# A hybrid decoder trunk: a reordered recurrence stage, a gate row broadcast by DMA, and a new spread of the conditioning products

## The chip, the cores and the metric

The kernel runs on one core of one Trainium2 chip. The metric is the device time of one execution in microseconds (us), the median of several executions. A core has five engines that this text names as the profile does: TensorE (PE, with its weight loads shown as PEld), VectorE (DVE), ScalarE (ACT), GpSimd (POOL) and SyncE (SP). In this kernel SP issues the transfers from memory; its queue is shown as SPq. Engines run side by side, each takes its own instructions strictly in the order of the compiled program, and they wait for each other through semaphores.

## The reference

Two layers are applied to a sequence of 256 tokens with 1024 features. Each layer has three sub-layers: a half-step SwiGLU FFN, a token mixer, and another half-step FFN. The mixer of layer 0 is HGRN2, a gated linear recurrence; that of layer 1 is a chunked causal gMLP. So there are six stages: ffn0, hg, ffn1, ffn2, gm, ffn3.

```python
def sublayer(x, fn, pre_g, post_g, shift, scale, gate, res_w):
    h = rms_norm(x, pre_g) * (1.0 + scale) + shift
    return x + res_w * gate * rms_norm(fn(h), post_g)

def swiglu(h, w_in, w_out):
    a, b = jnp.split(h @ w_in, 2, axis=-1)
    return (jax.nn.silu(a) * b) @ w_out

# HGRN2: q, f, i, g = split(h @ w_in); 8 heads of 128
#   f = lb + (1-lb) sigmoid(f), k = 1 - f, S_t = diag(f_t) S_{t-1} + k_t i_t^T, o_t = S_t^T silu(q_t)
#   out = (rms_norm(o per head) * silu(g)) @ w_out
```

The shift, scale and gate vectors of all stages come from `silu(c) @ ada_w`: per stage 24 columns of 128 features, 144 in all. The kernel computes each column as one product over a 128x1024 slab of `ada_w`; these are the conditioning products.

## The kernel before

The activations stay on chip, the weights (float32) are streamed once. Every weight block is 128x2048 and comes in two halves of 512 KB. `wblock` (L111 to L124) issues the two loads, ScalarE casts each half to a high part (L118) and VectorE subtracts it to get a low part (L119); TensorE then computes each product as three passes, high by high, high by low and low by high. There are twelve slots for these 128x2048 tiles (`whl`), four for raw halves.

`next_block` (L126) hands out the blocks in one fixed order and loads ahead by `self.ahead` blocks. The loads are kept in program order on SP's queue. `pace` (L133) spreads the conditioning products over the loads: `pace(upto, blocks)` lets each following block issue the same share of the products that are missing to `upto`. The table `bgs` (L925) has the count to which each stage goes. A product is a 512 KB load into one of the two slots of the pool `adap` (L165, L166) and one multiply-and-sum on VectorE (L168). `pre_cols` (L172) and `gate_tile` (L187) issue at once what is still missing of the columns that they read.

`gate_tile` (L187 to L200) makes G, the gate times the post-norm weight, as a 128x1024 tile with the same row in every partition: eight TensorE transposes of a broadcast column (L197) into two PSUM banks and two ScalarE copies (L199). `tail` (L248) uses G at the end of the stage (L257, L261).

An FFN stage runs units of hidden features (`unit`, L310), each from two blocks, with an output block behind (`out_unit`, L331), then the last three output blocks (`out_last`, L337) and the tail, in which the normalisation of the next stage begins. `ffn` calls `G_fn` at u == 8 of 11.

The stage hg (`hgrn`, L447) is written out by hand. `feat` (L455) projects 512 features with features on partitions, in four steps; `tok` (L472) projects 512 features with tokens on partitions, in four steps; `gate_f` (L486) turns a forget projection into decay sums with exponentials and logarithms, and borrows the slots of `adap` for its work tile L (L488). `attn` (L513) handles four heads: diagonal scores (L521), seven levels of halving, each with scaled copies X (L544 to L555), a set of score matmuls (L561) and a masked merge (L532), and then the output matmuls (L594, L596). `finish` (L601) normalises the outputs of four heads. `zip_steps` (L657) puts steps of other work between the steps of `attn` as fill for TensorE. The order before is: output gate of half 0 and values of half 0 together; queries of half 0; forget gate of half 0; G; queries of half 1 and one step of the forget gate of half 1 ahead; `attn(0)` beside the rest of that and the values of half 1; `attn(1)` beside the output gate of half 1, `finish(0)` and half of the output projection; then the silu of the second output gate, `finish(1)` and the tail. `self.gate` (L564) makes the next fill matmul follow the last score matmul in TensorE's order; `table` (L70) switches ScalarE's function table.

Of the kernel before, what the change touches and what calls it, by code (L numbers as in the profile page):

```python
# [10 lines left out]
F32 = mybir.dt.float32  # L11
# [4 lines left out]
ALU = mybir.AluOpType  # L16
# [17 lines left out]
class Body:  # L34
    def __init__(self, ctx, tc, ins, out):
        self.ctx, self.tc, self.nc, self.out = ctx, tc, tc.nc, out
        self.d = dict(zip(_INS, ins))
        pool = lambda name, bufs, **k: ctx.enter_context(tc.tile_pool(name=name, bufs=bufs, **k))
        self.const = pool("const", 1)
        self.raw = pool("raw", 4)  # L40
        self.whl = pool("whl", 12)
        self.act = pool("act", 1)
        self.adap = pool("adap", 2)
        self.cols = pool("cols", 2)
        self.tiny = pool("tiny", 4)
# [5 lines left out]
        self.yps = pool("yps", 1, space=PSUM)  # L51


    def load(self, out, src):
# [132 lines left out]
    def gate_tile(self, s, res_w):  # L187
        nc = self.nc
        self.ada(24 * s + 24)
        g = self.cols.tile([P, KC], F32, tag="gate", name="gate")  # L190
        nc.vector.tensor_add(g, self.mod[s][:, 16:24], self.adab[:, 24 * s + 16:24 * s + 24])
        nc.vector.scalar_tensor_tensor(g, g, res_w, self.npost[:, s, :], op0=ALU.mult, op1=ALU.mult)
        G = self.act.tile([P, D], F32, tag="G", name="G")
        for h in range(2):
            ps = self.acc.tile([P, 512], F32, tag="acc", name="gps")
            for k in range(4):
                nc.tensor.transpose(ps[:, k * P:(k + 1) * P], g[:, 4 * h + k:4 * h + k + 1].to_broadcast([P, P]),  # L197
                                    self.ident)
            nc.scalar.copy(G[:, h * 512:(h + 1) * 512], ps)  # L199
        return G  # L200


# [244 lines left out]
    def hgrn(self, hT, G_fn, pre_next, nxt, bg):  # L447
# [65 lines left out]
        def attn(hb, bank, res):  # L513
# [86 lines left out]

        def finish(hb, ops, sqrt=False):  # L601
            ss = self.tiny.tile([P, 8], F32, tag="ss8", name="ss8")
            o4 = [o.rearrange("p t h v -> p (t h) v") for o in ops]
            for u in range(2):
                for i in range(4):
                    junk = self.scr.tile([P, 512], BF16, tag="junka", name="junka")
                    nc.scalar.activation(junk[:, 0:P], o4[u][:, i, :], AF.Square, accum_out=ss[:, 4 * u + i:4 * u + i + 1])
            nc.vector.tensor_scalar(ss, ss, 1.0 / P, EPS, op0=ALU.mult, op1=ALU.add)
            r = self.tiny.tile([P, 8], F32, tag="r8", name="r8")
            if sqrt:  # L610
                self.tact(ss, ss, AF.Sqrt)
                nc.vector.reciprocal(r, ss)
# [1 line left out]
                self.rsqrt(r, ss)  # L614
            for u in range(2):
                pair = 2 * hb + u
                on = self.t2().rearrange("p (i v) -> p i v", i=4)
                for i in range(4):
                    t, c0 = i // 2, (2 * pair + i % 2) * P
                    nc.vector.scalar_tensor_tensor(on[:, i, :], o4[u][:, i, :], r[:, 4 * u + i:4 * u + i + 1],  # L620
                                                   gg[:, t, c0:c0 + P], op0=ALU.mult, op1=ALU.mult)
# [18 lines left out]
        def bank_a():  # L640
            return self.acc.tile([P, 512], F32, tag="acc", name="ab")

        def g_silu(g):
            o = gg[:, :, g * 512:(g + 1) * 512]
            self.tact(o, o, AF.Silu)

        def once(fn):
            fn()
            return
            yield  # L650

        def run(*gens):
            for gen in gens:
                for _ in gen:
                    pass
# [20 lines left out]
        v = self.wtile(F32).rearrange("p (t c) -> p t c", t=NT)  # L676
# [3 lines left out]
        kn, bq = [], [self.wtile(F32), self.wtile(F32)]  # L680
        qs = lambda hb, pr: bq[hb][:, H4 + 512 * pr:H4 + 512 * pr + 512]
        run(feat(lambda pr, ps: self.tact(qs(0, pr), ps, AF.Silu)))
        kn.append(self.wtile(F32))
# [4 lines left out]
        def q1_silu():  # L688
            self.table("silu_and_others")
            self.tact(bq[1][:, H4:], bq[1][:, H4:], AF.Silu)  # L690
            self.table("natural_log_exp_and_others")
        self.ahead = 1
        kn.append(self.wtile(F32))
        ops, oTs = [[], []], []
        G = G_fn()
        zip_steps(attn(0, bank_y, ops[0]), [
            feat(lambda pr, ps: nc.scalar.copy(qs(1, pr), ps)), once(q1_silu),
            feat(lambda pr, ps: gate_f(1, pr, ps)),
            tok(lambda t, ps: nc.scalar.copy(v[:, t, 512:], ps))], 5)
        self.ahead = 1  # L700
        oall = []
        y = None

        def outs():
            finish(0, ops[0])
            yield
            y = self.y_banks()
            state["y"] = y
# [11 lines left out]
        self.table("silu_and_others")  # L720
        g_silu(1)
        pre_next()
        self.table("sqrt_and_others")
        finish(1, ops[1], True)
# [190 lines left out]
    def run(self):  # L915
# [57 lines left out]
def _blk(w, rows, cols):  # L973

    r0, nr = rows
    c0, ncol = cols
    return w[r0:r0 + nr, c0:c0 + ncol].reshape(nr // P, P, ncol).transpose(1, 0, 2).reshape(P, -1)


def _layout(i):  # L980
# [35 lines left out]
    L["wffn"] = np.stack(wf)  # L1016
    hw, ho = a["hg_w_in"][0], a["hg_w_out"][0]
    bl = []
    for c0 in (3072, 2048, 0, 1024, 512, 1536, 2560, 3584):
        bl += [_blk(hw, (512 * h, 512), (c0, 512)) for h in range(2)]  # L1020
# [37 lines left out]
```

## Time and profile before

| what | value |
|---|---|
| median of 3 runs | 1213.34 us (1212.44 to 1213.79) |
| the profiled execution | 1208.2 us, its span from first to last instruction 1206.4 us |
| mean granted TensorE clock | 0.986 |
| TensorE busy | 1161.2 us, 96% of the span |
| VectorE busy | 858.4 us, 71% |
| ScalarE busy | 627.7 us, 52% |
| read from memory | 276.97 MB, 230 GB/s over the span |

A row of a windows view gives the stretch in us from the start of the span, its length, then for each engine the busy time with the number of instructions in brackets, then the granted clock (1.00 is full), the busy share of the DMA engines and the rate in GB/s. A row of waits names who waited, for whom, the total in us, how often and the longest. A row of the timeline gives start and length in us, engine, line, operation, and in square brackets the idle time before and what ended it. Matmuls overlap, so the distance of two starts is what one costs.

### The profile page before, as it was taken

The page shows a single profiled execution, that of the slowest core. Times are in us where ns is not written, and L with a number is a line of the kernel's source. Part 1 is how long each engine was busy: PE and PEld are TensorE (multiplying, and loading weights), DVE is VectorE, ACT ScalarE, POOL GpSimd, SP SyncE. Part 2 cuts the span into 40 slices and gives each one's busy share as a digit, 9 for nine tenths or more (in the row PEclk, how much of TensorE's full clock was granted, in tenths as well). Part 3 has the DMA queues.
Part 4 walks back from the last instruction along what each step waited for, and adds up shares of the span by engine and source line. Part 5 has one row for each costly group of instructions (what it writes and reads, how often), then busy time and mean ns, then how long its engine had stood idle before and what let it go on. Part 6 is the DMA issues. An engine that isn't in the chain of part 4 may idle for free.

```text
span 1206.4 us, 18818 instructions
## 1 busy us (share of the span) xinstructions
PE 1161.2 (96%) x7424; PEld 1042.9 (86%) x7424; DVE 858.4 (71%) x1223; ACT 627.7 (52%) x925; POOL 0.2 (0%) x4
## 2 busy tenths in 40 slices
PE   7999999999988999998899999999999999999997
PEld 6999997898876999986789999888888887999996
DVE  6998788879878877767766455466878787755632
ACT  6454446669576433334754344454654457534431
POOL 0000000000000000000000000000000000000000
PEclk9999999999998999998899999999999999999999
DMA  9888988863345888888667666436777665766630
GB/s 354 303 299 328 346 307 310 279 228 130 102 143 176 293 309 295 303 290 270 209 206 231 210 222 200 160 123 237 243 244 248 223 213 192 249 209 206 228 104 35
DMA packets 78714, 279.25 MB, mean 231 GB/s; under 512 B 9633, under 2 KB 10273, under 8 KB 78626
## 3 DMA queue, kind: packets, MB, share of 16 engines
q1 hardware_dynamic: 78626, 278.05, 67.7%
q8 instruction: 58, 0.95, 0.3%
q14 instruction: 30, 0.25, 0.1%
HBM read 276.97 MB, written 1.05 MB: 230 GB/s over the span
## 4 chain that ended last, share of the span: by engine, by line
PE 64%; DMA 17%; DVE 9%; ACT 5%; issue 4%; SPq 1%; DVEq 0%; ACTq 0%
DMA raw<-in_wffn 11%; PE ups L322 9%; PE ups L324 9%; PE ups L323 9%; PE y L141 6%; PE y L143 6%; PE y L142 6%; PE ups L389 4%; DVE w L119 3%; DMA ada<-in_ada 3%; ACT w L118 2%; DMA raw<-in_whg 2%; DVE junkv L168 2%; PE pps L289 2%; PE pps L290 2%
## 5 line engine op out<-in xcount | busy, mean ns | idle before, releaser
L118 ACT CAST w<-raw 128x1024 fp32r<-128x1024 f32 x376 | 389.1, 1049 | 385.7 <-DMA raw<-in_wffn 153.6
L119 DVE TENSOR_TENSOR w<-raw,w 128x1024 fp32r<-128x1024 f32 x376 | 454.2, 1222 | 168.1 <-ACT w L118 157.1
L322 PE MATMUL ups<-hhi,w 128*128 128x256 f32 x1280 | 363.4, 284 | 0.8 <-ACT w L118 0.7
L324 PE MATMUL ups<-hhi,w 128*128 128x256 f32 x1280 | 362.1, 283 | 1.1 <-DVE w L119 1.1
L323 PE MATMUL ups<-hlo,w 128*128 128x256 f32 x1280 | 361.8, 283 | 0.0
L322 PEld LDWEIGHTS ups<-hhi,w 128*128 128x128 f32 x1280 | 245.3, 192 | 3.0 <-ACT w L118 1.5
L323 PEld LDWEIGHTS ups<-hlo,w 128*128 128x128 f32 x1280 | 245.3, 192 | 1.7 <-issue 0.2
L324 PEld LDWEIGHTS ups<-hhi,w 128*128 128x128 f32 x1280 | 245.2, 192 | 1.6 <-DVE w L119 1.6
L168 DVE CUSTOM_DVE_ANT_0 junkv<-ada,cond 128x1024 bf16<-128x1024 f32 x144 | 175.8, 1221 | 44.5 <-DMA ada<-in_ada 43.5
L141 PE MATMUL y<-w,t 128*128 128x512 f32 x448 | 181.0, 404 | 2.0 <-ACT w L118 1.2
L142 PE MATMUL y<-w,t 128*128 128x512 f32 x448 | 179.9, 402 | 2.8 <-DVE w L119 2.8
L143 PE MATMUL y<-w,t 128*128 128x512 f32 x448 | 179.3, 400 | 0.1
L142 PEld LDWEIGHTS y<-w,t 128*128 128x128 f32 x448 | 85.2, 190 | 23.6 <-DVE w L119 5.6
L141 PEld LDWEIGHTS y<-w,t 128*128 128x128 f32 x448 | 85.6, 191 | 21.4 <-ACT w L118 1.9
L143 PEld LDWEIGHTS y<-w,t 128*128 128x128 f32 x448 | 85.4, 191 | 20.6 <-DVE t L147 0.4
L289 PE MATMUL pps<-w,hhi 128*128 128x512 f32 x160 | 65.2, 407 | 5.9 <-DVE hhi L245 5.9
L290 PE MATMUL pps<-w,hhi 128*128 128x512 f32 x160 | 64.2, 402 | 0.0
L355 DVE TENSOR_TENSOR t<-t,ups 128x512 f32<-128x512 f32 x38 | 25.9, 685 | 31.5 <-PE ups L324 31.3
L146 ACT CAST t<-t 128x512 fp32r<-128x512 f32 x50 | 30.8, 618 | 29.0 <-DVE t L355 24.9
L292 PE MATMUL pps<-w,hlo 128*128 128x512 f32 x160 | 43.2, 391 | 0.0
L289 PEld LDWEIGHTS pps<-w,hhi 128*128 128x128 f32 x160 | 31.0, 194 | 13.9 <-DVE hhi L245 3.8
L324 PE MATMUL fps<-hhi,w 128*128 128x256 f32 x128 | 36.5, 285 | 1.7 <-DVE w L119 1.7
(190 smaller groups left out, 1215.7 us busy)
## 6 DMA issues: line engine op xcount, KB each, us to landing
raw<-in_wffn SPq DMA_DIRECT2D x264, 512.0 KB, 5.5
ada<-in_ada SPq DMA_DIRECT2D x144, 512.0 KB, 6.0
raw<-in_wgmu SPq DMA_DIRECT2D x48, 512.0 KB, 5.1
raw<-in_whg SPq DMA_DIRECT2D x40, 512.0 KB, 6.0
raw<-in_wgmv SPq DMA_DIRECT2D x24, 512.0 KB, 4.5
t<-in_gbin SPq DMA_DIRECT2D x6, 256.0 KB, 5.1
x<-in_x SPq DMA_DIRECT2D x2, 512.0 KB, 4.1
out<-x SPq DMA_DIRECT2D x4, 256.0 KB, 2.0
```

Of the source, the lines that this page charges most:

```text
L118: nc.scalar.copy(hi[:, sl], raw)
L119: nc.vector.tensor_sub(lo[:, sl], raw, hi[:, sl])
L141: self.paced(mm(ps, l[0], r[0], start=start, stop=False))
L142: mm(ps, l[0], r[1], start=False, stop=False)
L143: mm(ps, l[1], r[0], start=False, stop=stop)
L168: nc.vector.tensor_tensor_reduce(junk, t, self.cond, 1.0, 0.0, ALU.mult, ALU.add, self.mod[i // 24][:, i % 24:i % 24 + 1])
L289: mm(res[g][t], h(0, kc), u(0, kc), start=kc == 0, stop=False)
L290: mm(res[g][t], h(0, kc), u(1, kc), start=False, stop=False)
L322: self.paced(mm(o, u[0], h[0], start=start, stop=False))
L323: mm(o, u[0], h[1], start=False, stop=False)
L324: mm(o, u[1], h[0], start=False, stop=stop)
L389: nc.tensor.matmul(res[i][:, c * S:(c + 1) * S], wb[u // 2][:, c0:c0 + P], hT[u % 2][:, :, kc, :], start=kc + c + u == 0, stop=kc == KC - ...
```

## The change

Three parts.

1. `gate_tile` transposes the 128x8 gate once into 8x128, copies it to SBUF, writes it as 4 KB to a tile in device memory and reads it back with a broadcast to 128 partitions; both transfers are issued by GpSimd.
2. In `hgrn`, both halves of the output gate are projected first, then the forget gate of half 0, then both halves of the queries; the values of half 0 become fill (two steps ahead of `attn(0)`, two inside it), beside the whole forget gate of half 1 and one step of the values of half 1, whose other three steps go beside `attn(1)`. `G_fn` moves behind `attn(0)`. `once` now takes one step of a generator. The fill is also ordered behind the diagonal scores. `outs` has one more empty step behind `finish(0)`. `finish` squares a whole bank at a time, multiplies outputs and gate from PSUM on VectorE, sums the squares there and scales by the norm at the end. The silu of the second output gate and two table switches at the end of the stage are gone, and the blocks of `whg` are laid out in the new order.
3. `bgs` becomes 46, 64, 92, 118, 138, 144 (it was 48, 64, 112, 120, 136, 144).

```diff
+        ps = self.acc.tile([P, 512], F32, tag="acc", name="gps")
+        nc.tensor.transpose(ps[0:KC, 0:P], g, self.ident)
+        row = self.cols.tile([KC, P], F32, tag="grow", name="grow")
+        nc.scalar.copy(row, ps[0:KC, 0:P])
+        flat = self.dram.tile([KC, P], F32, tag="gflat", name="gflat")
+        nc.gpsimd.dma_start(flat, row)
         G = self.act.tile([P, D], F32, tag="G", name="G")
-        for h in range(2):
-            ps = self.acc.tile([P, 512], F32, tag="acc", name="gps")
-            for k in range(4):
-                nc.tensor.transpose(ps[:, k * P:(k + 1) * P], g[:, 4 * h + k:4 * h + k + 1].to_broadcast([P, P]),
-                                    self.ident)
-            nc.scalar.copy(G[:, h * 512:(h + 1) * 512], ps)
+        nc.gpsimd.dma_start(G, flat.rearrange("k p -> (k p)").unsqueeze(0).to_broadcast([P, D]))
...
-                    nc.tensor.matmul(ps[:, i * P:(i + 1) * P], k[:, c], q[:, c], start=True, stop=True)
+                    score = nc.tensor.matmul(ps[:, i * P:(i + 1) * P], k[:, c], q[:, c], start=True, stop=True)
+                self.gate = score
...
+            og = self.t4()
             for u in range(2):
-                for i in range(4):
-                    junk = self.scr.tile([P, 512], BF16, tag="junka", name="junka")
-                    nc.scalar.activation(junk[:, 0:P], o4[u][:, i, :], AF.Square, accum_out=ss[:, 4 * u + i:4 * u + i + 1])
+                o3 = ops[u].rearrange("p t h v -> p (t h) v")
+                sq = self.t2().rearrange("p (i v) -> p i v", i=4)
+                nc.scalar.activation(sq, o3, AF.Square)
+                c0 = 2 * (2 * hb + u) * P
+                nc.vector.tensor_mul(og[:, 512 * u:512 * u + 512].rearrange("p (t c) -> p t c", t=NT),
+                                     ops[u].rearrange("p t h v -> p t (h v)"), gg[:, :, c0:c0 + 2 * P])
+                nc.vector.reduce_sum(ss[:, 4 * u:4 * u + 4], sq, axis=mybir.AxisListType.X)
...
-                    nc.vector.scalar_tensor_tensor(on[:, i, :], o4[u][:, i, :], r[:, 4 * u + i:4 * u + i + 1],
-                                                   gg[:, t, c0:c0 + P], op0=ALU.mult, op1=ALU.mult)
+                    nc.vector.tensor_scalar(on[:, i, :], on[:, i, :], r[:, 4 * u + i:4 * u + i + 1], None, op0=ALU.mult)
...
         for t in range(NT):
-            self.tact(gg[:, t, 0:512], pg[0][t], AF.Silu)
-            nc.scalar.copy(v[:, t, 0:512], pg[1][t])
+            for g in range(2):
+                self.tact(gg[:, t, 512 * g:512 * g + 512], pg[g][t], AF.Silu)
...
-        run(feat(lambda pr, ps: self.tact(qs(0, pr), ps, AF.Silu)))
...
         run(feat(lambda pr, ps: gate_f(0, pr, ps)))
+        self.table("silu_and_others")
+        for hb in range(2):
+            run(feat(lambda pr, ps: self.tact(qs(hb, pr), ps, AF.Silu)))
+        self.table("natural_log_exp_and_others")
...
+        val = lambda i: tok(lambda t, ps: nc.scalar.copy(v[:, t, 512 * i:512 * i + 512], ps))
+        v0, v1 = val(0), val(1)
+        zip_steps(attn(0, bank_y, ops[0]), [
+            once(v0), once(v0), feat(lambda pr, ps: gate_f(1, pr, ps)), v0, once(v1)], 2)
         G = G_fn()
-        zip_steps(attn(0, bank_y, ops[0]), [
-            feat(lambda pr, ps: nc.scalar.copy(qs(1, pr), ps)), once(q1_silu),
-            feat(lambda pr, ps: gate_f(1, pr, ps)),
-            tok(lambda t, ps: nc.scalar.copy(v[:, t, 512:], ps))], 5)
...
             finish(0, ops[0])
+            yield
             yield
...
-        zip_steps(attn(1, bank_a, ops[1]), [
-            tok(lambda t, ps: nc.scalar.copy(gg[:, t, 512:], ps)), outs()], 0)
+        zip_steps(attn(1, bank_a, ops[1]), [v1, outs()], 0)
         y = state["y"]
-        self.table("silu_and_others")
-        g_silu(1)
...
-        bgs = {"ffn0": 48, "hg": 64, "ffn1": 112, "ffn2": 120, "gm": 136, "ffn3": 144}
+        bgs = {"ffn0": 46, "hg": 64, "ffn1": 92, "ffn2": 118, "gm": 138, "ffn3": 144}
```

More of the change, by code (lines that the diff above doesn't have):

```diff
@@ L51, in __init__ @@
         self.yps = pool("yps", 1, space=PSUM)
+        self.dram = pool("dram", 2, space=bass.MemoryType.DRAM)
     def load(self, out, src):
@@ L602, in finish @@
             ss = self.tiny.tile([P, 8], F32, tag="ss8", name="ss8")
-            o4 = [o.rearrange("p t h v -> p (t h) v") for o in ops]
+            r = self.tiny.tile([P, 8], F32, tag="r8", name="r8")
+            og = self.t4()
             for u in range(2):
-                for i in range(4):
-                    junk = self.scr.tile([P, 512], BF16, tag="junka", name="junka")
-                    nc.scalar.activation(junk[:, 0:P], o4[u][:, i, :], AF.Square, accum_out=ss[:, 4 * u + i:4 * u + i + 1])
+                o3 = ops[u].rearrange("p t h v -> p (t h) v")
[5 more added lines that the diff above has]
+                nc.vector.reduce_sum(ss[:, 4 * u:4 * u + 4], sq, axis=mybir.AxisListType.X)
             nc.vector.tensor_scalar(ss, ss, 1.0 / P, EPS, op0=ALU.mult, op1=ALU.add)
-            r = self.tiny.tile([P, 8], F32, tag="r8", name="r8")
             if sqrt:
@@ L641, in bank_a, with once @@
             return self.acc.tile([P, 512], F32, tag="acc", name="ab")
[L643 to L650, printed above, removed]
+        def once(gen):
+            yield next(gen)
         def run(*gens):
@@ L715, in outs @@
                     yield
-        zip_steps(attn(1, bank_a, ops[1]), [
-            tok(lambda t, ps: nc.scalar.copy(gg[:, t, 512:], ps)), outs()], 0)
+        zip_steps(attn(1, bank_a, ops[1]), [v1, outs()], 0)
         y = state["y"]
-        self.table("silu_and_others")
-        g_silu(1)
         pre_next()
@@ L1018, in _layout @@
     bl = []
-    for c0 in (3072, 2048, 0, 1024, 512, 1536, 2560, 3584):
-        bl += [_blk(hw, (512 * h, 512), (c0, 512)) for h in range(2)]
+    for c0, h in ((3072, 0), (3072, 1), (3584, 0), (3584, 1), (1024, 0), (1024, 1), (0, 0), (0, 1), (512, 0), (512, 1),
+                  (2048, 0), (1536, 0), (1536, 1), (2048, 1), (2560, 0), (2560, 1)):
+        bl.append(_blk(hw, (512 * h, 512), (c0, 512)))
     bl += [_blk(ho, (256 * u, 256), (0, D)) for u in range(4)]
```

11 lines of the change are left out of this document (3 added, 8 removed).

## The prediction

> **What bounds the kernel now.** I read the page first, then stretches of 20 us, then who waits where TensorE falls behind, and last the load queue, which stands behind most of it.
>
> ```profile
> span 1206.4 us, 18818 instructions
> 440.00:460.00 20.00, 20.00 (x147) 18.91 (x146) 14.84 (x20) 7.43 (x8) 0.00 (x0) 1.00 0.84 285
> 560.00:580.00 20.00, 16.78 (x53) 10.80 (x52) 14.79 (x15) 14.27 (x16) 0.00 (x0) 0.83 0.80 268
> 340.00:360.00 20.00, 17.85 (x107) 15.21 (x106) 16.39 (x18) 16.15 (x30) 0.00 (x0) 1.00 0.57 185
> 360.00:380.00 20.00, 15.62 (x64) 11.95 (x64) 14.27 (x29) 11.34 (x24) 0.00 (x0) 0.83 0.46 158
> ```
>
> The first row under the span is how most of the kernel looks: TensorE without a gap at full clock. So the time is the sum of TensorE's matmuls and the places where it starves. The other rows are the two places: the end of ffn1 (560 to 580) and the end of hg (340 to 380). In both the granted clock falls to 0.83 as well.
>
> The price of the first place can be read directly. Here are the output matmuls that close ffn1 and, below, the same 96 in ffn2:
>
> ```profile
> 553.20:592.30 39.10, 30.41 (x96) 20.69 (x96) 2.05 (x3) 2.03 (x6) 0.83 0.69 230
> 763.00:786.60 23.60, 22.84 (x96) 17.78 (x96) 2.05 (x3) 2.07 (x6) 1.00 0.37 120
> ```
>
> 39.1 against 23.6 us: ffn1 loses **15.5 us** that ffn2 does not lose. The stages compute the same; what differs is the conditioning products, 112 - 64 = 48 against 120 - 112 = 8. The load queue's own waits in the steady part, ffn1 first, then ffn2:
>
> ```profile
> SPq L55 <- DVE mod L168: 54.6, 32, 2.8
> SPq L55 <- DMA ada<-in_ada: 38.7, 24, 3.6
> ...
> SPq L55 <- DVE w L119: 108.0, 47, 4.5
> ```
>
> ```profile
> 407.00:540.00 133.00, 132.89 (x950) 124.73 (x947) 99.37 (x136) 50.23 (x59) 0.00 (x0) 1.00 0.88 299
> 622.00:755.00 133.00, 133.00 (x954) 125.31 (x953) 77.19 (x84) 56.87 (x68) 0.00 (x0) 1.00 0.67 218
> ...
> raw<-in_wffn SPq DMA_DIRECT2D x40, 512.0 KB, 7.3
> ada<-in_ada SPq DMA_DIRECT2D x36, 512.0 KB, 5.3
> ```
>
> In ffn2 the queue waits for weight slots: it is ahead. In ffn1 it never waits for those; it stands behind a product's load, whose two slots are still landing or being multiplied: 54.6 + 38.7 = 93.3 us for the 36 products of these 133 us (last two rows, of that window), 2.6 us each. The other 39.7 us over 40 halves are 2.0 us per block. With r products per block the queue needs 2.0 + 2.6r per block. TensorE eats one in 48 matmuls of 0.12 us (rows below), 5.8 us, so the queue falls behind above **r = 1.45**.
>
> **The products.** ffn1 had 48 over 26 blocks, r = 1.85, 6.8 us a block: behind from the start, until the loads made ahead are used up at its end. Afterwards ffn1 has 28 (1.08), ffn2 26 (1.0), gm 20 over 30 (0.67), ffn0 30 over 25 (1.2, before 1.28): all under 1.45. ffn0 shows that 1.28 holds:
>
> ```profile
> 62.00:195.00 133.00, 133.00 (x910) 123.22 (x909) 110.60 (x147) 65.67 (x75) 0.00 (x0) 1.00 0.91 324
> SPq L55 <- DVE w L119: 34.1, 23, 3.5
> ...
> 195.00:212.00 17.00, 14.46 (x63) 11.35 (x62) 15.70 (x31) 12.37 (x26) 0.00 (x0) 0.96 0.82 272
> ```
>
> No idle time in 133 us, and the queue waits for weight slots (34.1 us), but the change of stage behind it idles 17.00 - 14.46 = 2.5 us with VectorE at 15.7 of 17; ffn2's end, with few products, idles 0.8 of 23.6. So the 15.5 us of ffn1 will not come back whole, and ffn2 pays for its 18 new products. I take 1.5 us left in ffn1 and 1.0 more in ffn2: **-13.0 us**; bounds -15.5 (nothing left) and -8 (both ends idle 2.5 and the slow clock doubles it in one). VectorE's sum is untouched, the products only move: 18 times 1.22 us (L168 below) into ffn2, where it works 77 of 133 us.
>
> **The gate row.** Eight transposes on TensorE become one, six times:
>
> ```profile
> 257.60 0.28 PE L323 MATMUL fps<-hlo,w 128*128 128x256 f32 x1
> 257.72 0.28 PE L324 MATMUL fps<-hhi,w 128*128 128x256 f32 x1
> 257.84 1.03 PE L197 MATMUL gps<-ident,gate 128*128 128x128 f32 x8
> 259.58 0.36 PE L322 MATMUL fps<-hhi,w 128*128 128x256 f32 x1 [0.70 <-DVE shift L181]
> ...
> 1149.15 0.58 ACT L199 COPY G<-gps 128x512 f32<-128x512 f32 x1
> 1188.51 0.68 DVE L257 TENSOR_TENSOR yg<-y,G 128x512 f32<-128x512 f32 x1
> ```
>
> Eight take 1.03 - 0.27 of overlap = 0.76 us from first to last start, so one costs 0.11 and seven fewer 0.76; six times that is **-4.5 us**, all in stretches where TensorE is never idle otherwise. ScalarE copies 8x128 instead of two banks of 0.58 us. New are two chained transfers from GpSimd's queue, on which nothing else stands; the trace has no such transfer. From below: no delay. From above: the slowest median landing here, 7.3 us, twice, 15 us. The shortest cover is the last stage's, 1149.2 to 1188.5, 39 us (hg's G, moved behind `attn(0)`, still has all of `attn(1)` and the end of hg). So it costs nothing in time; without cover, each us late would hold `tail` and with it the next stage, six times. The 0.5 MB per stage are one load among some 90.
>
> The Trainium skill, "SBUF — State Buffer", its section on the two sides of SBUF, speaks against this path: GpSimd writes the descriptors of its own transfers, and a VectorE instruction in a 2-port mode locks it out, so that a transfer of about 0.62 us takes 3.1. By that page the two transfers would be some 6 us, an estimate from its figures, and the sum would stay. No run here shows it yet.
>
> **The recurrence.** Moved: 8 projections, the same matmuls in another order. I go through the places where TensorE waits in hg now.
>
> ```profile
> PE fps L324 <- DVE w L119: 1.7, 2, 1.5
> 276.30:320.00 43.70, 41.69 (x304) 38.52 (x303) 40.10 (x63) 36.34 (x71) 0.00 (x0) 1.00 0.35 117
> ...
> 250.26 0.33 SPq L55 DMA_DIRECT2D ada<-in_ada  x1
> 250.68 0.92 SPq L55 DMA_DIRECT2D raw<-in_whg  x2
> 263.65 0.33 SPq L55 DMA_DIRECT2D ada<-in_ada  x1
> ...
> SPq L55 <- DVE w L505: 12.0, 1, 12.0
> ...
> 238.31 0.86 SPq L55 DMA_DIRECT2D raw<-in_whg  x2
> ...
> 255.28 0.59 ACT L491 ACTIVATE L<-fps 128x512 f32<-128x512 f32 x1
> ...
> raw<-in_whg SPq DMA_DIRECT2D x40, 512.0 KB, 6.0
> ...
> L118 ACT CAST w<-raw 128x1024 fp32r<-128x1024 f32 x376 | 389.1, 1049 | 385.7 <-DMA raw<-in_wffn 153.6
> L119 DVE TENSOR_TENSOR w<-raw,w 128x1024 fp32r<-128x1024 f32 x376 | 454.2, 1222 | 168.1 <-ACT w L118 157.1
> L168 DVE CUSTOM_DVE_ANT_0 junkv<-ada,cond 128x1024 bf16<-128x1024 f32 x144 | 175.8, 1221 | 44.5 <-DMA ada<-in_ada 43.5
> ```
>
> (a) Before `attn(0)` TensorE waits 1.7 us for the low part of the forget weights of half 1, because the queue stood still for 12.0 us: product 64 wanted a slot of `adap` that `gate_f(0)` held as L until L505, and the next weights stood behind it. In the new order `gate_f(0)` comes one projection (11.5 us: 96 matmuls at 0.12) earlier, while hg's share of products rises from 16 to 18 over nine blocks. Four products, two behind each of weight blocks 9 and 10, then follow L in program order, and **the standstill moves from the forget weights of half 1 to the second block of the queries of half 1**. The first L is held from 255.3 to 263.6 now; 11.5 us earlier frees it at 252, the second half a projection (5.8 us) later at 258. The block behind lands 6.0 us after that and takes 2.3 us to cast and subtract (rows above): 266. TensorE wants it 1.4 us into that projection, which starts where G's transposes stand now: 257.8 + 1.4 = 259.2. Bounds: 0, if the compiler's planner hands the slots to the products first, and 7 us. I take 3, nearer to 0 because L need not start as late as now; with the 1.7 gone, +1.3 net. (b) The 0.7 us before 259.58 go with G's banks: -0.7, bounds -0.7 and 0.
>
> (c) `attn(0)`: VectorE works 40.1 of 43.7 us, TensorE idles 2.0. ScalarE loses two table switches there; VectorE gains half a forget gate's work beside it and loses nothing. 0, bounds -2 and +3. `attn(1)` has one fill step less and two steps without fill; VectorE has more room there. +0.5, bounds 0 and +2.5.
>
> (d) The end of hg:
>
> ```profile
> 347.48 1.28 ACT L72 ACT_TABLE_LOAD   x1
> ...
> 354.21 0.28 ACT L607 ACTIVATE junka<-ab 128x128 bf16<-128x128 f32 x1 [2.50 <-PE ab L596]
> ...
> 358.92 0.28 ACT L607 ACTIVATE junka<-ab 128x128 bf16<-128x128 f32 x1
> ...
> PE y L142 <- DVE w L119: 2.8, 7, 0.8
> ...
> 363.19 1.93 PE L625 MATMUL ots<-ident,t 128*128 128x128 f32 x7 [5.14 <-DVE t L620]
> ```
>
> TensorE idles 5.14 us while eight squares, with weight casts between them, take ScalarE from 354.2 to 359.2. Two squares of a bank (a ScalarE copy of that size took 0.58 us, L199) end about 3 us sooner. VectorE adds a product and a sum per bank (0.68 each by L257); the last two, 1.4 us, lie on the path, against which stands that the sums wait behind fewer casts, 1 us by L118. The silu and its two tables were done by 349, off this path: 0. Net -2.5, bounds -4.5 (nearly all of the idle time) and +0.5.
>
> The granted clock is 0.83 in the slice with this gap. The skill's page "TensorE: Matmul & The Clock Gate", Part 1, puts the half clock behind about 3.4 us of idleness; by that a gap cut to 2.6 us would spare the slow stretch as well and the sum would be 1 us better. The trace disagrees: in ffn1's end (540 to 592) TensorE's waits for L119 are at most 0.8 us each (the row above), and the clock is 0.83 there too. I leave it out.
>
> Sum of hg: 1.3 - 0.7 + 0 + 0.5 - 2.5 = **-1.4 us**, bounds -9 and +11.
>
> **Sum.** -13.0 - 4.5 - 1.4 = -18.9 us. The profiled execution took 1208.2 us (span 1206.4 plus 1.8), so 1189.3 there; it lay 5.1 us under the median of the runs, from which the same difference gives **1194.4 us**.
>
> **The rivals.** *The standstill bites (0.20).* In (a) the full 7 us, (c) +5.5, (d) nothing gained: hg +10 instead of -1.4, 1206 us. For it: the wait of 12.0 exists, VectorE is at 92% in `attn(0)`. Against: 13 us of lead of the loads at that point (block 9 is issued at 238.3 and used at 259.6) and the planner's freedom. *hg gains all (0.10).* No wait in (a), (d) at its bound: hg -7, 1189 us. *The products cure half (0.06).* ffn1's end keeps half its 15.5 us, because the compiled order of its tail was made for the old timing: -7 instead of -13, 1200 us. Against it stands ffn2, the same code without the loss. *G comes late (0.04), the other side.* If the two transfers took 45 us instead of under 15, each of six tails would wait 6 us: +36, 1230 us; it decides against the change from 39 + 21.3/6 = 42.6 us on. For it: GpSimd's queue is untried here, and the skill's lock (above). Against: a factor of three over the slowest landing. *The change does nothing (0.02):* the products are issued elsewhere than `pace` says; ffn1 keeps its loss, 1207.
>
> **How the numbers follow.** The forecast has 0.58. About 2.4 us, 0.2%, is what a measurement can tell from no change. The forecast's own cases lie between 1188 and 1201. Range 1185 to 1206: from nearly all bounds at their gain (-15.5, -4.5 and -9 make 1184) up to the first rival; the late G, the change that does nothing and the upper edge of the first rival, under 0.2, are left out. Faster 0.92 (all but the late G and parts of the first and last rival), the same 0.03, slower 0.05.
>
> **What would show it.** Products: between ffn1's last units and ffn2, 96 output matmuls in about 25 us at clock near 1.00, and the queue of ffn1 and ffn2 waiting for L119. Gate row: six transposes, none idle before `tail` on G. hg: a wait of the second query projection's matmuls for L119 near 259 (my standstill), or none; 2 to 3 us before the transposes of `finish(1)`. Wrong would be a wait of `tail` on a transfer, a loss at the end of ffn2 as large as ffn1's now, or `attn` with more idle time than 3 us.

## The result, and the profile after

The changed kernel takes 1224.71 us, the median of 4 runs (1222.07 to 1227.38), against 1213.57 us for the kernel before, measured beside it: a ratio of 1.0093, 95% interval 1.0067 to 1.0119. It is **slower by 11 us**, where the forecast said 19 us faster. The profiled execution took 1223.24 us.

Lines moved in the changed file: L118 and L119 became L119 and L120, L168 became L169, L555 and L561 became L558 and L564, L620 and L625 became L626 and L630. In the kernels with own slots (the experiments below) they stand one line further, in the other test kernels a line or two off.

The windows view of both kernels, cut where the first projection of each stage starts: hg and ffn1. Before:

```profile
210.40:381.40 171.00, 158.65 (x1032) 142.46 (x1032) 139.65 (x233) 120.33 (x226) 0.00 (x0) 0.97 0.52 173
381.40:592.30 210.90, 201.41 (x1256) 179.11 (x1257) 161.64 (x221) 97.85 (x134) 0.00 (x0) 0.96 0.83 281
```

After:

```profile
209.60:407.20 197.60, 172.81 (x1025) 154.76 (x1026) 145.38 (x246) 112.45 (x193) 1.08 (x2) 0.88 0.46 154
407.20:602.80 195.60, 190.88 (x1249) 173.48 (x1250) 135.59 (x178) 94.34 (x130) 1.07 (x2) 1.00 0.75 256
```

ffn1 is 15.3 us shorter and **hg 26.6 us longer**; of the other stages, cut in the same way, ffn0 is 0.8 us shorter and ffn2, gm and ffn3 are 2.1, 1.3 and 1.2 longer. The two profiled executions differ by 15.1 us and the medians by 11.1, so stage differences carry some us of chance. The hg row splits its loss in two. TensorE's idle time grew from 171.00 - 158.65 = 12.4 to 197.60 - 172.81 = 24.8 us. Its busy time grew by 14.2 us with seven matmuls fewer (1025 for 1032): the granted clock fell from 0.97 to 0.88. Half the loss is waiting, half is matmuls that run slowly.

**ffn1 did what the forecast said.** The 96 output matmuls that close ffn1 (a window of tile y, after); those of ffn2 take 23.6 us as before:

```profile
577.90:602.80 24.90, 22.64 (x96) 17.84 (x96) 2.03 (x3) 2.04 (x6) 1.00 0.40 130
```

The load queue's waits in ffn1's steady part:

```profile
SPq L56 <- DVE w L120: 86.7, 45, 5.9
SPq L56 <- DVE mod L169: 4.2, 4, 1.3
SPq L56 <- DMA ada<-in_ada: 2.2, 1, 2.2
```

24.9 us for 39.1, full clock, and the queue waits for weight slots (86.7 us) and hardly for products (4.2 + 2.2, for 93.3 before).

What the forecast did not have is a new wait 28 us into ffn2, 3.02 us long, in a stage in which TensorE before never waited longer than 1.2 us:

```profile
630.76 0.62 PE L142 MATMUL y<-w,t 128*128 128x512 f32 x1 [3.02 <-ACT t L147]
```

**hg.** The waits of TensorE in it, after, are mainly 9.0 us for `finish` (two waits), 6.8 for the scaled copies X of `attn` (three) and 3.1 for the queries (one). In order of time, rows of the timeline:

```profile
263.20 2.08 PE L523 MATMUL ab<-w 128*128 128x128 f32 x8 [3.12 <-ACT w L79]
266.00 0.58 PE L324 MATMUL fps<-hhi,w 128*128 128x256 f32 x1 [0.73 <-ACT w L119]
286.42 0.39 PE L326 MATMUL fps<-hhi,w 128*128 128x256 f32 x1 [0.76 <-DVE w L120]
290.74 3.67 PE L564 MATMUL ab<-t 128*128 128x64 f32 x16 [2.45 <-DVE t L558]
355.50 1.30 PE L630 MATMUL ots<-ident,t 128*128 128x128 f32 x5 [3.11 <-DVE t L626]
389.20 1.94 PE L630 MATMUL ots<-ident,t 128*128 128x128 f32 x8 [5.93 <-DVE t L626]
```

Before there were 5.14 us at the end and no other wait above 2.1 us. Now TensorE waits at the start of `attn(0)` (263), inside it (284 to 294), at `finish(0)` (355) and as long as ever at `finish(1)` (389). And behind these waits the clock is halved (windows just behind four of them):

```profile
263.00:269.20 6.20, 5.27 (x23) 4.98 (x24) 5.06 (x8) 2.72 (x4) 0.00 (x0) 0.50 0.75 278
290.70:297.00 6.30, 6.26 (x31) 6.26 (x32) 3.95 (x6) 3.18 (x11) 0.00 (x0) 0.54 0.62 230
355.00:362.00 7.00, 6.50 (x32) 6.43 (x33) 5.25 (x14) 5.63 (x7) 0.00 (x0) 0.50 0.00 0
389.00:396.00 7.00, 6.80 (x21) 5.31 (x22) 3.88 (x11) 1.37 (x2) 0.00 (x0) 0.54 0.79 255
```

The load queue around the first wait, rows of the timeline:

```profile
240.05 1.64 SPq L56 DMA_DIRECT2D raw<-in_whg  x2
253.37 5.72 SPq L56 DMA_DIRECT2D ada<-in_ada  x2
259.14 0.90 SPq L56 DMA_DIRECT2D raw<-in_whg  x2
```

And its longest wait there:

```profile
SPq L56 <- DVE w L507: 13.3, 2, 11.6
```

From 241.7 to 253.4 SP stands behind a product whose slot is held as L until L507, and the next weights leave at 259.1. That is the standstill that the forecast placed there, "frees it at 258", about 1 us later. TensorE's wait beside it is another than forecast: 3.12 us for the queries of ScalarE and only 0.73 for weights.

### The profile page after: what moved, and what is told of

Its sections match the earlier page's. It is cut to its first block, busy times and chain, and to the rows that moved or that the text cites. A ratio compares the mean times of both kernels' runs of the same rounds, so it can differ in the third digit from the quotient of the medians.

```text
span 1221.5 us, 18672 instructions
## 1 busy us (share of the span) xinstructions
PE 1164.2 (95%) x7382; PEld 1047.7 (86%) x7382; DVE 857.6 (70%) x1231; ACT 614.2 (50%) x888; POOL 6.8 (1%) x16
## 4 chain that ended last, share of the span: by engine, by line
PE 72%; DMA 11%; DVE 7%; ACT 6%; issue 3%; SPq 0%; DVEq 0%; ACTq 0%
PE ups L324 11%; PE ups L325 11%; PE ups L326 11%; PE y L142 7%; PE y L144 7%; PE y L143 7%; DMA raw<-in_whg 4%; PE ups L391 4%; DMA ada<-in_ada 3%; DMA raw<-in_wffn 3%; DVE w L120 3%; ACT w L119 3%; PE ab L564 2%; PE pps L144 1%; PE pps L143 1%
## 5 line engine op out<-in xcount | busy, mean ns | idle before, releaser
L119 ACT CAST w<-raw 128x1024 fp32r<-128x1024 f32 x376 | 387.5, 1048 | 358.8 <-PE ups L325 122.2
L120 DVE TENSOR_TENSOR w<-raw,w 128x1024 fp32r<-128x1024 f32 x376 | 452.8, 1220 | 118.3 <-ACT w L119 111.4
L169 DVE CUSTOM_DVE_ANT_0 junkv<-ada,cond 128x1024 bf16<-128x1024 f32 x144 | 175.8, 1221 | 94.6 <-DMA ada<-in_ada 94.1
L144 PE MATMUL y<-w,t 128*128 128x512 f32 x448 | 177.7, 398 | 0.1
L142 PEld LDWEIGHTS y<-w,t 128*128 128x128 f32 x448 | 84.8, 189 | 23.6 <-ACT t L147 5.6
L291 PE MATMUL pps<-w,hhi 128*128 128x512 f32 x160 | 62.8, 396 | 6.2 <-DVE hhi L247 6.2
L292 PE MATMUL pps<-w,hhi 128*128 128x512 f32 x160 | 62.6, 391 | 0.0
```

The source lines that it names most:

```text
L119: nc.scalar.copy(hi[:, sl], raw)
L120: nc.vector.tensor_sub(lo[:, sl], raw, hi[:, sl])
L142: self.paced(mm(ps, l[0], r[0], start=start, stop=False))
L144: mm(ps, l[1], r[0], start=False, stop=stop)
L169: nc.vector.tensor_tensor_reduce(junk, t, self.cond, 1.0, 0.0, ALU.mult, ALU.add, self.mod[i // 24][:, i % 24:i % 24 + 1])
L291: mm(res[g][t], h(0, kc), u(0, kc), start=kc == 0, stop=False)
```

## The experiments

Ratios are to the kernel before. Lengths of hg are rows of the windows view, from the first projection of hg to that of ffn1. They come from single profiles, and the repeats below show that a stage with many waits varies by up to 3.8 us between executions; smaller differences of hg are read only together with the medians. The kernel before, measured beside the others each time, had medians of 1211.5 to 1212.7 us here and 1213.6 beside the changed kernel, so a step between two medians below can be off by 1 to 2 us.

**The products alone**: the kernel before with the new `bgs`.

```diff
-bgs = {"ffn0": 48, "hg": 64, "ffn1": 112, "ffn2": 120, "gm": 136, "ffn3": 144}
+bgs = {"ffn0": 46, "hg": 64, "ffn1": 92, "ffn2": 118, "gm": 138, "ffn3": 144}
```

> The kernel before with only the new spread of the conditioning products. Theory 1 (the spread is worth what the end of ffn1 lost, and the old order of hg bears two more products): the 96 closing matmuls of ffn1 take about 25 us instead of 39.1, the time falls by 10 to 15 us, to 1199 to 1203. Rival (the spread harms hg, because 18 instead of 16 products stand in front of its weights): hg gets 5 us or more longer, and the time falls by less than 8.

1209.15 us, ratio 0.998 (0.9949 to 1.0012): no difference that can be told. Windows, hg:

```profile
210.90:390.20 179.30, 162.44 (x1032) 146.30 (x1032) 139.37 (x236) 118.58 (x224) 0.00 (x0) 0.94 0.50 164
```

The largest new wait of TensorE in it:

```profile
PE fps L322 <- DVE A L182: 3.7, 1, 3.7
```

The load queue there, by the timeline:

```profile
249.21 7.85 SPq L55 DMA_DIRECT2D ada<-in_ada  x3
257.16 27.48 SPq L55 DMA_DIRECT2D raw<-in_whg  x8
```

The rival held. ffn1 gained its 15 us (195.7 for 210.9), hg gave 8.3 back, and ffn2, gm and ffn3 are 2.4, 3.0 and 1.6 us longer. Two products less in ffn0 are two more in hg, and they take turns with the two L of `gate_f(0)` in the two slots of `adap`: three products leave between 249.2 and 257.1, and no weights in that time. The matmuls of the row in the middle wait until VectorE has read out what `gate_f(0)` had in PSUM, late by the same turns.

**Own slots for L, with the products alone.**

```diff
+        self.lp = pool("lp", 2)
-            L = self.adap.tile([P, 512], F32, tag="ada", name="L")
+            L = self.lp.tile([P, 512], F32, tag="L", name="L")
```

> The kernel before with the new spread of the products and two own slots for L. Theory 1 (in the spread alone, hg loses 8 us because products and L take turns in the two slots of adap): hg's idle and slow time goes from 29 back to 22 us or less, and the time falls to 1198 to 1204. Rival (the 18 products crowd the load queue itself, slots or not): hg stays above 26 us and the time above 1207.

1204.62 us, ratio 0.9945 (0.9920 to 0.9970). Windows, hg:

```profile
212.10:385.20 173.10, 160.72 (x1033) 144.04 (x1033) 139.20 (x237) 118.36 (x224) 0.00 (x0) 0.96 0.52 170
```

hg is back to 173.1 us and ffn1's gain stays (194.7). The shared slots were nearly the whole price of the products in hg, and this small edit **beats both kernels**. The step from the products alone is 4.5 us by the medians; the two intervals overlap, so it rests on hg's 6.2 us as well. The time lies just above the 1198 to 1204 us that were expected.

**Own slots in the changed kernel.** The same edit.

> The changed kernel with two slots of its own for the forget gate's work tile L, so that no product waits for L. Theory 1 in the form that the standstill of the load queue behind L makes the weights of the queries and of the second forget gate late: the queue no longer stands still near 241 to 259, the waits before attn(0) and in its first steps (about 14 us of TensorE's time between 259 and 294) shrink to under 4, and the time falls by 8 to 14 us, to 1211 to 1217. Rival (VectorE and ScalarE are simply full there, or the diagonal scores stand too early in TensorE's order): the waits move by less than 4 us.

1218.02 us, ratio 1.0035 (1.0011 to 1.0059): 6.7 us better than the changed kernel, a little less than the 8 to 14 expected, and still slower than before. Windows, hg, from the slowest of its ten executions (1223.14 us):

```profile
209.40:398.00 188.60, 167.96 (x1025) 151.82 (x1025) 145.47 (x246) 112.64 (x193) 1.07 (x2) 0.91 0.49 161
```

TensorE's waits in it:

```profile
PE ots L631 <- DVE t L627: 9.6, 2, 6.5
PE ab L565 <- ACT t L80: 4.2, 1, 4.2
PE ab L565 <- DVE t L559: 3.4, 2, 2.4
```

The waits for weights are gone, and so is that at 263: with L out of `adap`, the compiled order has the diagonal scores behind the projections and not inside the second query projection. Left are 4.2 us at the first level of `attn(0)`, where ScalarE's exponentials come behind the silus of the queries, a table load and three weight casts, and both waits of `finish`. The first of these waits alone is longer than the 4 us that were expected for all waits up to there. The freed queue and the other order of TensorE come together in this edit; no run separates them.

**A second profile of the kernel before, and of the kernel just shown.** No edit.

> The kernel before, unchanged, for a second profile. If stage lengths can be compared between single profiles, each of the six lies within 1.5 us of the first profile's 210.4, 171.0, 210.9, 194.3, 221.0, 198.8 us; where one differs by more, differences of that size between other profiles say nothing.

> The changed kernel with own slots for L, unchanged, for a second profile. In its first profile a wait of 2.41 us in attn(0) was followed by 6.6 us at a granted clock of 0.50; in the kernel that has the old norm besides, the same matmuls after a wait of 2.42 us ran at 1.00. Theory: the half clock belongs to the place and what went before it, so the second profile shows it at the same places again, the clock of hg at 0.90 to 0.92 and hg at 187 to 190 us. Rival: it falls by chance from one execution to the next: one of the half-speed stretches of the first profile is missing or a new one is there, and hg differs by 3 us or more.

The stages of the kernel before came out 210.3, 170.5, 208.2, 193.7, 221.7 and 199.5 us: five within 0.7 us, ffn1 off by 2.7, so the expectation failed there. The hg of the changed kernel with own slots came out 184.8 for 188.6 us, at 1217.22 us in all. Here is the place in question, windows from the same matmuls on; first profile:

```profile
313.70:320.30 6.60, 6.55 (x24) 5.91 (x25) 5.11 (x6) 1.76 (x2) 0.00 (x0) 0.50 0.26 82
```

Second profile, the wait by the timeline:

```profile
312.76 1.97 PE L565 MATMUL ab<-t 128*128 128x64 f32 x16 [2.42 <-DVE t L559]
```

and the windows behind it:

```profile
312.70:315.10 2.40, 2.34 (x19) 2.29 (x20) 2.40 (x4) 1.78 (x2) 0.00 (x0) 1.00 0.04 7
315.10:318.50 3.40, 3.40 (x10) 2.62 (x9) 3.24 (x3) 0.00 (x0) 0.00 (x0) 0.50 0.61 169
```

The rival held: the same wait is followed by 6.6 us of half clock in one execution and by 3.4 us, which begin 2.3 us later, in the other.

**The recurrence alone**: order, fill and norm of the changed kernel, with the old products and the old gate row.

> The changed order of the recurrence and the new norm alone, with the gate row and the spread as before. Theory 1 (the new order is what costs): 20 to 30 us slower than before, 1234 to 1243, since the end of ffn1 keeps its loss as well. Rival (order and spread only hurt together, because 18 products stand in front of the queries' weights): within 8 us of before.

1222.78 us, ratio 1.0065 (1.0045 to 1.0086): slower by 8 us by the ratio and 10 by the medians, far under the theory and at the edge of its rival; ffn1 keeps its loss (212.2 us). Windows, hg:

```profile
209.90:393.70 183.80, 166.06 (x1033) 150.24 (x1033) 143.14 (x242) 114.27 (x195) 0.00 (x0) 0.92 0.49 161
```

hg +12.8. With +8.3 of the products and +3.4 of the gate row (next) that makes 24.5 of the 26.6 us: the parts nearly add up, as far as single profiles can tell.

**The gate row alone**, and the gate row on top of the best kernel.

```diff
-            for k in range(4):
-                nc.tensor.transpose(ps[:, k * P:(k + 1) * P], g[:, 4 * h + k:4 * h + k + 1].to_broadcast([P, P]),
-                                    self.ident)
+        nc.tensor.transpose(ps[0:KC, 0:P], g, self.ident)
...
+        nc.gpsimd.dma_start(G, flat.rearrange("k p -> (k p)").unsqueeze(0).to_broadcast([P, D]))
```

> The kernel before with only the gate row made by one transpose and two transfers from GpSimd. Theory 1: 42 transposes less, 4 to 5 us faster, about 1209. Rival (the transfers or the other instruction order cost something): no gain or slower, with a wait on G or on the load queue that the kernel before does not have.

> The same with the gate row by one transpose and two transfers. Theory 1 (the gate row lost its gain through the timing of adap's slots in hg and through the full load queue of ffn1, both gone here): 3 to 5 us faster than the run without it. Rival (the gate row costs by itself, through its transfers or the changed order of instructions): the same or slower than without it.

Alone 1217.32 us, ratio 1.0033 (1.0011 to 1.0055), which excludes a gain; on top of the best kernel 1204.71 us for 1204.62, ratios 0.9931 (0.9899 to 0.9963) and 0.9945, which by itself would not exclude 4.5 us. The 4.5 us showed in neither median. Windows of the first, hg:

```profile
211.10:385.50 174.40, 159.02 (x1025) 142.29 (x1025) 139.65 (x233) 119.53 (x225) 1.07 (x2) 0.97 0.52 173
```

TensorE has seven matmuls fewer in hg and idles 3.0 us more, in several places, each wait at most 1.3 us longer than before. On top of the best kernel hg is 177.7 us for 173.1. Both profiles have hg longer by about what all six stages were to save, but that is hardly more than two executions of one kernel differ by. That G comes late is excluded; the DMA issues on the changed kernel's page:

```profile
G<-gflat POOLq DMA_DIRECT2D x6, 512.0 KB, 6.3
```

The small transfer ahead of each takes 3.8 us at the median, so the two together some 10 us, within the 15 that the forecast allowed. No matmul and no product with G waited for them. Where the saved 0.76 us per stage go isn't settled; stage lengths of single profiles are too coarse for it.

**The new norm alone**: the kernel before with the new `finish`.

```diff
-                for i in range(4):
-                    nc.scalar.activation(junk[:, 0:P], o4[u][:, i, :], AF.Square, accum_out=ss[:, 4 * u + i:4 * u + i + 1])
+                nc.scalar.activation(sq, o3, AF.Square)
+                nc.vector.tensor_mul(og[...], ops[u]..., gg[:, :, c0:c0 + 2 * P])
+                nc.vector.reduce_sum(ss[:, 4 * u:4 * u + 4], sq, axis=mybir.AxisListType.X)
```

> The kernel before with only the new norm (finish). Theory 1 (ScalarE's square root stands behind a weight cast that waits for its load, so that the shorter squares gain nothing): the wait before the last transposes stays at 5 to 6.5 us and the time within 2 us of before. Rival (the new norm is 2.5 us shorter, as predicted, and only the new order hides it): the wait falls to 3 us or less.

1216.17 us, ratio 1.0013 (0.9989 to 1.0037): in the old order no difference that can be told. Windows, hg:

```profile
211.40:388.50 177.10, 163.97 (x1033) 147.59 (x1033) 143.03 (x242) 116.75 (x198) 0.00 (x0) 0.94 0.51 167
```

TensorE's waits for the norm:

```profile
PE ots L627 <- DVE t L623: 6.8, 2, 5.0
```

The wait at `finish(1)` stays at 5.0 us for 5.1: the norm doesn't shorten what it was to shorten. A second wait comes at `finish(0)` (6.8 in 2), with the clock at 0.66 from 339 to 348 us around it, so that hg's busy time is 5.3 us up for 0.8 us of idle time.

**The old norm (the last diff undone), or an earlier empty step, in the changed kernel with own slots.** The diff is the second:

```diff
+            yield
             finish(0, ops[0])
-            yield
             yield
```

> The changed kernel with own slots for L and the empty step of outs moved ahead of finish(0). Theory 1 (the transposes of finish(0) stand in TensorE's order before the norm is ready, since one fill step fewer lies before them; TensorE waits 3.3 us and then runs at the slow clock): the wait before them goes, hg gets 4 to 7 us shorter than with own slots alone. Rival (a step without fill costs the same wherever it stands): under 2 us.

> The changed kernel with own slots for L, and the old per-head output norm (eight squares of 128 columns) put back; the gate row, the products and the order of the projections stay as changed. Theory 1: with own slots the wait ahead of the transposes of finish(0) (3.27 us, and slow matmuls behind it) comes from the new norm, whose gated products and sums stand in VectorE's order ahead of the scalings; with the old norm that wait is under 1 us, hg falls from 188.6 to 182 to 186 us and the time lies 3 to 6 us under the 1218.0 us of the kernel with own slots. Rival: the step without fill ahead of it is to blame: the wait stays above 2.5 us, hg at 187 to 190, the time within 1.5 us of 1218.

With the empty step ahead of `finish(0)` 1214.90 us, ratio 1.0022 (1.0002 to 1.0043), and hg 184.2, but the wait stays: the theory failed, and against own slots without the step (1.0035, hg 188.6 and 184.8) no gain can be told. With the old norm 1207.31 us, ratio 0.9969 (0.9945 to 0.9994); windows, hg and the matmuls behind the wait of 2.42 us:

```profile
209.80:387.30 177.50, 160.23 (x1025) 144.89 (x1025) 141.96 (x239) 116.19 (x223) 1.08 (x2) 0.94 0.51 171
314.30:320.70 6.40, 6.34 (x44) 5.88 (x45) 5.66 (x6) 1.75 (x2) 0.00 (x0) 1.00 0.39 115
```

**10.7 us by the medians, 8 by the ratios**, more than the 3 to 6 expected; the two intervals do not overlap. In hg it is 11.1 us against the first profile with own slots and 7.3 against the second. The wait at `finish(0)` is gone without any fill having been moved; the one at `finish(1)` stays, 7.1 us. The half clock of 314 to 320 in that first profile is missing here behind an equal wait (1.00 for 0.50); it is worth some 3 us, half of 6.6, and may be chance. How the norm delays `finish(0)` is seen in the changed kernel's timeline of VectorE:

```profile
352.44 0.69 DVE L547 TENSOR_TENSOR t<-w 128x512 f32<-128x512 f32 x1 [1.13 <-PE ab L564]
353.05 0.16 DVE L97 TENSOR_TENSOR rs_q<-rs_y 128x8 f32<-128x8 f32 x1
...
354.40 0.16 DVE L100 SCALAR_TENSOR_TENSOR r<-rs_q,rs_y 128x8 f32<-128x8 f32 x1
...
355.08 1.65 DVE L626 TENSOR_SCALAR t<-t,r 128x128 f32<-128x128 f32 x8
```

The last steps of the root stand behind L547 of `attn(1)`, which waits for TensorE's scores; the root ends at 354.6, L626 starts at 355.1, and TensorE, whose next instructions are the transposes of L626's output, stands still from 352.4 to 355.5. The lateness begins in ScalarE's order, where both squares stand behind a copy that waits for matmuls of `attn(1)`; the changed kernel's timeline:

```profile
343.41 0.59 ACT L587 COPY t<-ab 128x512 f32<-128x512 f32 x1 [3.88 <-PE ab L584]
343.89 1.09 ACT L611 ACTIVATE t<-ab 128x512 f32<-128x512 f32 x2
```

With the old norm the eight squares ran ahead of that copy (323.9 to 330.2, the copy at 331.2). The sums are in `ss` at 332.2 there and at 339.0 with own slots and the new norm, 6.8 us apart, where TensorE's score matmuls ahead of the transposes are 2.6 us apart (338.25 and 340.85). From the sums on, the root takes about 6 us in both.

**The order alone**: the new order, with its fill and table switches, with new products and own slots, but the old norm and gate row, and the empty step first.

> The order of the projections of the changed kernel with the new products and own slots for L, but the old output norm, the old gate row of eight transposes, and the step without fill set ahead of finish(0). It differs from the old order with new products and own slots (1204.6 us, hg 173.1 us) in the order of the projections alone. Theory 1: the order itself costs, because attn(0) now begins inside the second query projection and waits for exponentials that ScalarE makes behind the silus of the queries and their table loads: hg 178 to 183 us, 1209 to 1214 us. Rival: once L has its own slots the order costs nothing: hg 171 to 175 us, 1203 to 1206 us.

1209.28 us, ratio 0.9977 (0.9949 to 1.0004). Windows, hg:

```profile
211.30:388.30 177.00, 162.13 (x1033) 146.06 (x1033) 139.58 (x237) 116.14 (x221) 0.00 (x0) 0.94 0.50 166
```

Its new wait of TensorE:

```profile
PE ab L563 <- DVE t L557: 4.6, 2, 4.3
```

4.7 us more than the old order (1204.62; the intervals overlap a little), hg 177.0 for 173.1, with a wait of 4.3 us at the first level of `attn(0)` that the old order doesn't have. That wait, 4.0 to 4.4 us, is in all five profiles of the new order with own slots. So the new order costs by itself, by these figures somewhat less than the shared slots (6.7) and the norm (10.7).

## Why the prediction was wrong

The steps down from the changed kernel, by medians and by hg: own slots 1224.7 to 1218.0 (197.6 to 188.6), old norm to 1207.3 (177.5), old gate row and earlier empty step 1209.3 (177.0), old order 1204.6 (173.1). The step that failed is the sum of hg, -1.4 us with a bound of +11: hg lost 26.6. It failed in (a), (c) and (d), where waits came at other places or for other engines than forecast, and because the slow matmuls behind waits stood at nothing. The two other terms, products and gate row, came out smaller than forecast.

**Products, -13.0: the mechanism right, the size too large.** ffn1 -15.3 and ffn2 +2.1 make -13.2 us in the changed kernel's profile. But five profiles here have the old products and nine the new ones, and their means say more: ffn1 211.4 and 195.8, ffn2 193.4 and 197.5, gm 221.3 and 223.9, ffn3 199.4 and 200.7, ffn0 within 0.3. Outside hg the products are worth 8.0 us. The forecast gave ffn2 1.0 us, where 4.0 came, most of it the wait at 630 above (2.3 to 3.6 us in all nine profiles with the new products, in none of the five with the old), and gm, which got four products more, nothing, where 2.6 came; in ffn2 and gm every profile with the new products is longer than every one with the old. And the two products moved from ffn0 into hg were counted only inside step (a): they cost 8.3 us of hg by themselves, in the old order too, which the forecast had not priced.

**(a), +1.3: the place right, the wait another.** At the place itself TensorE lost 3.9 us (3.12 + 0.73), near the 3 that were taken, but mostly to the queries on ScalarE and not to weights, and 6.2 us at half clock followed. "Nearer to 0 because L need not start as late as now" failed. L took a slot of `adap` and so had to wait for a product itself; first L at 245.9 us, by the profile of tile L:

```profile
L493 ACT ACTIVATE L<-fps x4: 573/597/597, 245.9 to 308.6; 128x512 f32<-128x512 f32 x4
```

Load, product and L wait for each other in turn, and the lateness doesn't end at the first block: weights are late again at 286. I priced one block and no slow clock; own slots gave back 6.7 us, together with the other order of TensorE.

**(c), 0 and +0.5: failed.** It went by VectorE's load in `attn(0)`. What decides is the order in ScalarE. In the changed kernel the silus of the queries stand behind the late exponentials of `gate_f(0)` and a table load, and the diagonal scores wait 3.12 us for them at 263; with own slots the first exponentials of `attn(0)` stand behind those silus, the next table load and weight casts, and TensorE waits 4.0 to 4.4 us. "ScalarE loses two table switches there" was a misreading: the loads at 275.0 and 277.3 us became loads at 261.3 and 282.8, still around the start of `attn(0)`; the whole kernel has one load fewer, 17 for 18, the one at the end of hg. "VectorE has more room" in `attn(1)` failed as well: the wait at 355 is for VectorE.

**(d), -2.5: failed.** The wait became 5.93 us for 5.14. The squares did end early, but the square root didn't. ScalarE at the end of hg:

```profile
382.15 0.60 ACT L611 ACTIVATE t<-ab 128x512 f32<-128x512 f32 x1 [0.74 <-PE ab L599]
382.65 1.98 ACT L119 CAST w<-raw 128x1024 fp32r<-128x1024 f32 x2
386.38 1.04 ACT L119 CAST w<-raw 128x1024 fp32r<-128x1024 f32 x1 [1.75 <-DMA raw<-in_wffn]
387.33 0.20 ACT L79 ACTIVATE ss<-ss 128x8 f32<-128x8 f32 x1
```

And VectorE's last step ahead of the root:

```profile
385.19 0.16 DVE L616 TENSOR_SCALAR ss<-ss 128x8 f32<-128x8 f32 x1
```

The squares are done at 382.75, the root runs at 387.33. Of these 4.6 us the first 2.6 go to VectorE's products, sums and a weight subtraction between them; the last 2.0 are the third weight cast, which waits 1.75 us for its load with the root queued behind it. I had counted the casts between the squares and not those behind them. And the same edit acts twice: `finish(0)` was not in my sum, though that is where it costs most.

**The gate row, -4.5: not found in either test.** That its transfers hide was right; what the step from fewer matmuls to less time missed stays open.

**The slow clock** was left out of the sum on the ground that short waits showed it too. That was a reason to put it in: every new wait is to be priced with the slow matmuls behind it, and here these made 14.2 of 26.6 us. The rival *standstill bites* had the place and a part of the cause, at 1206 us; it left out the norm's cost and too priced waits by their length alone.

## What to carry to other kernels

Don't let a computed tile borrow the slots of a pool that loads fill: an in-order load queue then waits for compute, and everything behind it in the queue waits too. Two lines of code for own slots turned an edit that could not be told from neutral into a gain of 0.55%. When an operation gets shorter, look what stands behind it in its engine's order up to the consumer, at every place where the edit acts; and price waits of TensorE, several short ones too, with about as much again for the clock. That is an average: added up over the twelve profiles of other kernels, hg has 60 us more idle time of TensorE than in the kernel before and 63 us more busy time. Single profiles scatter widely (0.4 us busy for 3.0 idle with the gate row alone, 5.3 for 0.8 with the norm alone).

## What the runs showed of the hardware

The half clock comes behind waits well under 3.4 us, and not in the same way each time: after 2.4 us once 6.6 us of it, once 3.4 us with a delay of 2.3, once none. It also follows several waits of under 1 us each: at the end of ffn1 in the kernel before, six waits of 0.17 to 0.75 us, 2.3 us together, lie between 562 and 568.9 us, and the next 6.6 us ran at 0.50. The Trainium skill, "TensorE: Matmul & The Clock Gate", Part 1, states a window of about 3.4 us that runs free of the kernel; the stretches of 3.4 and 6.6 us are about one and two such windows, and a window that runs free would explain the differing start. That part of the Trainium skill puts the half clock behind a whole idle window; the waits here are shorter, so these traces disagree with that.

Twenty-five executions of the kernel before lay between 1205.0 and 1218.6 us, far wider than the first runs shown, so that single times decide nothing below 1% here.
